# Nearest-neighbour upsampling by two: eight drains ahead of the second load, and a single row copied behind the other 53

## The chip, the core and the metric

The kernel runs on one core of a Trainium2 chip. The metric is the device time of one execution in microseconds (us). A lower time is better. The kernel before takes 197.13 us, the median of three runs (197.12 to 197.26).

## What is computed

The input `x` is float32 with the shape (16, 64, 64, 64), which is 16.78 MB. The output doubles height and width, so it has the shape (16, 64, 128, 128) and 67.11 MB. Every input value is written four times:

```
new_h, new_w = (h * scale_factor, w * scale_factor)      # scale_factor is 2
for i in range(new_h):
    for j in range(new_w):
        result[:, :, i, j] = x[:, :, i // scale_factor, j // scale_factor]
```

There is no arithmetic. The work is to bring 16.78 MB in, to repeat it fourfold on the chip, and to bring 67.11 MB out.

## The kernel before

Batch, channel and height are flattened to 65,536 input rows of 64 values. Each of the 128 partitions holds 512 of these rows. All 512 rows of a partition fit into the on-chip memory at once, together with some free space, in one tile called `mem`. The input part of it is `xt`.

**Loads.** SyncE issues three loads, cut at the rows 0, 32, 288 and 512 of each partition. They are called load 1 (1 MB), load 2 (8 MB) and load 3 (7 MB) below. `begin_before_barrier` moves load 1 ahead of the barrier with which the program starts. Ahead of each load stand as many SyncE drains as `PAUSES` says: none, two and forty. The drains wait for nothing here; they let time pass between two issues.

**Copies.** VectorE expands the rows in nine groups of `rows = [54, 38, 54, 60, 54, 62, 64, 62, 64]`. A copy reads a row of 64 values with every value taken twice and the row taken twice, and writes 256 values. So 53 rows are 13,568 values in each partition, and one row is 256. The first group is split: the single row 0 is copied on its own as soon as load 1 is there, and then the rows 1 to 53 in a second copy. Row 53 lies in load 2, so this second copy waits for load 2.

**Places.** Even groups are written at the start of `mem`. Odd groups are written further on, and they end over input rows that earlier copies have already read. Therefore the copy of the second group (38 rows) waits until the copies of the first group have finished, and each copy from the third on waits until the store of two groups earlier has landed.

**Stores.** Each group is one store. SyncE issues the first, the second and the last store, behind its three loads and in the same queue (q1 in the profile). ScalarE issues the other six (q10). The stores of the first group and load 3 are thus neighbours in one queue: the first store's data can only move when load 3's data has been moved, and only if the store has been issued early enough. It is issued when both copies of the first group are done.

**End.** `close_early` rewrites the closing instructions so that most of the clean-up happens before the last store has landed. The change does not touch it.

Of the kernel before, what the change touches and what calls it, by code (L numbers as in the profile page):

```python
# [7 lines left out]


EARLY = 1  # L10
PAUSES = (0, 2, 40)


def begin_before_barrier(nc):
# [140 lines left out]
@with_exitstack  # L155
def kernel(
    ctx: ExitStack,
    tc: tile.TileContext,
    x: bass.AP,
    scale_factor: int,  # L160
    out: bass.AP,
):
    nc = tc.nc
    nc.at_finalize(begin_before_barrier)
    nc.at_finalize(close_early)
    P = nc.NUM_PARTITIONS
    s = int(scale_factor)
    B, C, H, W = x.shape
    R = B * C * H // P
    fdt = x.dtype  # L170

    xp = x.rearrange("b c h w -> (b c h) w").rearrange("(p r) w -> p r w", p=P)
    op = out.rearrange("b c (h hd) w -> (b c h) (hd w)", hd=s).rearrange(
        "(p r) w -> p r w", p=P
    )

    rows = [54, 38, 54, 60, 54, 62, 64, 62, 64]
    GROW = s * s
    FREE = 79
    WF = FREE * GROW * W
    assert sum(rows) == R
    mem_pool = ctx.enter_context(tc.tile_pool(name="mem", bufs=1))
    LEAD = 32
    whole = mem_pool.tile([P, LEAD + WF + R * W], fdt, name="mem")
    mem = whole[:, LEAD:]  # L190
    xt = mem[:, WF:].rearrange("p (r w) -> p r w", r=R)

    HEAD = 32
    cuts = [0, HEAD, R // 2 + HEAD, R]
    for n, (lo, hi) in enumerate(zip(cuts, cuts[1:])):
        for _ in range(PAUSES[n]):
            nc.sync.drain()  # L199
        nc.sync.dma_start(out=xt[:, lo:hi], in_=xp[:, lo:hi])  # L200

    def expanded(r0, r1):
        return (
            xt[:, r0:r1].unsqueeze(2).unsqueeze(4).to_broadcast([P, r1 - r0, s, W, s])
        )

    r0 = 0
    before = (0, 0)
    for n, k in enumerate(rows):
        size = k * GROW * W  # L210
        at = 0 if n % 2 == 0 else WF + r0 * W - size
        assert at >= before[1] or at + size <= before[0]
        before = (at, at + size)
        u = mem[:, at : at + size].rearrange(
            "p (k a w b) -> p k a w b", k=k, a=s, w=W
        )
        k0 = 1 if n == 0 else 0
        if k0:
            nc.vector.tensor_copy(out=u[:, :k0], in_=expanded(r0, r0 + k0))  # L219
        nc.vector.tensor_copy(out=u[:, k0:], in_=expanded(r0 + k0, r0 + k))  # L220
        issuer = nc.sync if n in (0, 1, len(rows) - 1) else nc.scalar
        issuer.dma_start(out=op[:, r0 : r0 + k, :], in_=u)
        r0 += k
# [35 lines left out]
```

## Time and profile before

| what | value |
|---|---|
| time, median of three runs | 197.13 us |
| time of the profiled execution | 197.12 us |
| its span, first to last instruction | 195.8 us |
| VectorE busy | 76.9 us (39%) |
| bytes read and written | 16.78 MB and 67.11 MB |
| mean rate of the DMA engines over the span | 428 GB/s |
| first store issued at | 38.35 us |

The span is 1.3 us shorter than the time of the same execution; what lies outside it is before the first or after the last instruction of the profile. In the rows of the profile, DVE is VectorE, SPq and ACTq are the queues of SyncE and ScalarE, and L220 is a line of the kernel. A row of a DMA view gives what moved in a stretch of time. A packet is counted whole in the stretch in which it starts. That is a nuisance for short stretches where rates are wanted, and a help where starts are to be counted: the rate times the length of the stretch, divided by the size of a packet, is the number of packets that started in it. For load 3 a packet is one partition's 57,344 bytes, for the first store one partition's 55,296 bytes, and for loads and stores of 64 rows it is 65,536 bytes. Each of the 16 DMA engines moves the packets of 8 partitions, one behind the other.

### The profile page before, as it was taken

The page shows a single profiled execution, that of the slowest core. Times are in us where ns is not written, and L with a number is a line of the kernel's source. Part 1 is how long each engine was busy: PE and PEld are TensorE (multiplying, and loading weights), DVE is VectorE, ACT ScalarE, POOL GpSimd, SP SyncE. Part 2 cuts the span into 40 slices and gives each one's busy share as a digit, 9 for nine tenths or more (in the row PEclk, how much of TensorE's full clock was granted, in tenths as well). Part 3 has the DMA queues.
Part 4 walks back from the last instruction along what each step waited for, and adds up shares of the span by engine and source line. Part 5 has one row for each costly group of instructions (what it writes and reads, how often), then busy time and mean ns, then how long its engine had stood idle before and what let it go on. Part 6 is the DMA issues. An engine that isn't in the chain of part 4 may idle for free.

```text
span 195.8 us, 118 instructions
## 1 busy us (share of the span) xinstructions
DVE 76.9 (39%) x10; POOL 0.2 (0%) x4
## 2 busy tenths in 40 slices
DVE  0000099990029287059008805920690079000000
POOL 0000000000000000000000000000000000000000
DMA  9999989889898998999999899999999999999994
GB/s 428 428 428 428 402 375 562 375 361 531 373 435 382 517 407 361 542 402 402 402 503 441 361 542 415 415 415 415 428 428 428 428 415 454 537 475 422 428 428 214
DMA packets 1728, 83.89 MB, mean 428 GB/s; under 512 B 192, under 2 KB 192, under 8 KB 192
## 3 DMA queue, kind: packets, MB, share of 16 engines
q10 hardware_dynamic: 864, 46.66, 55.0%
q1 hardware_dynamic: 864, 37.22, 44.3%
HBM read 16.78 MB, written 67.11 MB: 428 GB/s over the span
## 4 chain that ended last, share of the span: by engine, by line
DMA 61%; DVE 24%; issue 0%; SPq 0%
DMA out_dram<-mem 49%; DVE mem L220 24%; DMA mem<-in_x_dram 12%; SPq L199 0%
## 5 line engine op out<-in xcount | busy, mean ns | idle before, releaser
L220 DVE COPY mem<-mem 128x13824 f32<-128x13824 f32 (+5 forms) x9 | 76.6, 8515 | 84.8 <-DMA out_dram<-mem 65.8
L219 DVE COPY mem<-mem 128x256 f32<-128x256 f32 x1 | 0.3, 293 | 4.7 <-DMA mem<-in_x_dram 4.7
L240 POOL MEMSET const-bfloat16-1.0<- 128x1 bf16 x1 | 0.1, 101 | 0.0
L240 POOL MEMSET const-uint8-127<- 128x1 uint8 x1 | 0.1, 101 | 0.0
L240 POOL MEMSET const-float32-1.0<- 128x1 f32 x1 | 0.1, 100 | 0.0
L240 POOL MEMSET const-float32-0.0<- 128x1 f32 x1 | 0.1, 98 | 0.2 <-issue 0.2
## 6 DMA issues: line engine op xcount, KB each, us to landing
out_dram<-mem ACTq DMA_DIRECT2D x2, 7936.0 KB, 31.6
out_dram<-mem ACTq DMA_DIRECT2D x2, 6912.0 KB, 23.7
out_dram<-mem ACTq DMA_DIRECT2D x1, 7680.0 KB, 26.1
mem<-in_x_dram SPq DMA_DIRECT2D x1, 7168.0 KB, 37.7
out_dram<-mem SPq DMA_DIRECT2D x1, 6912.0 KB, 19.1
out_dram<-mem SPq DMA_DIRECT2D x1, 4864.0 KB, 25.4
mem<-in_x_dram SPq DMA_DIRECT2D x1, 1024.0 KB, 4.7
mem<-in_x_dram SPq DMA_DIRECT2D x1, 23.1
```

What stands on the lines that cost most here:

```text
L219: nc.vector.tensor_copy(out=u[:, :k0], in_=expanded(r0, r0 + k0))
L220: nc.vector.tensor_copy(out=u[:, k0:], in_=expanded(r0 + k0, r0 + k))
L240: nc = _bacc.Bacc("TRN2", target_bir_lowering=False, num_devices=1)
```

## The change

Two things change. `PAUSES` goes from `(0, 2, 40)` to `(0, 8, 40)`, so SyncE runs eight drains ahead of load 2 instead of two. And in the first group the single row moves: the copy of 53 rows comes first and covers the rows 0 to 52, and the single row is now row 53, copied behind it.

```
-PAUSES = (0, 2, 40)
+PAUSES = (0, 8, 40)
...
-        k0 = 1 if n == 0 else 0
-        if k0:
-            nc.vector.tensor_copy(out=u[:, :k0], in_=expanded(r0, r0 + k0))
-        nc.vector.tensor_copy(out=u[:, k0:], in_=expanded(r0 + k0, r0 + k))
+        parts = ((0, k - 1), (k - 1, k)) if n == 0 else ((0, k),)
+        for a, b in parts:
+            nc.vector.tensor_copy(out=u[:, a:b], in_=expanded(r0 + a, r0 + b))
```

On VectorE the order of the first two copies is reversed. Before, at the start of VectorE's program (128x256 is the single row, 128x13568 the 53 rows; DMAHW0 and DMAHW1 are the semaphores of load 1 and load 2, DVE is VectorE's own):

```order
L219 COPY mem<-mem 128x256 [waits DMAHW0_49]
L220 COPY mem<-mem 128x13568 [waits DMAHW1_49]
L220 COPY mem<-mem 128x9728 [waits DVE_49]
L220 COPY mem<-mem 128x13824 [waits DMAHW3_49]
L220 COPY mem<-mem 128x15360 [waits DMAHW4_49,DVE_49]
```

The same place of the changed program:

```order
L219 COPY mem<-mem 128x13568 [waits DMAHW1_49,DMAHW0_49]
L219 COPY mem<-mem 128x256
L219 COPY mem<-mem 128x9728 [waits DVE_49]
L219 COPY mem<-mem 128x13824 [waits DMAHW3_49]
L219 COPY mem<-mem 128x15360 [waits DMAHW4_49,DVE_49]
```

The large copy now reads rows of both loads, so it waits for two semaphores where it waited for one; a copy with two waits stands behind a separate wait instruction that holds the first of them. The single row waits for nothing of its own and follows the large copy. All later copies, and the order on SyncE and ScalarE, are as before, apart from the six added drains on SyncE between load 1 and load 2.

## The prediction

> **What bounds the kernel now.** I read the page first, for the engines' shares.
>
> ```profile
> DVE 76.9 (39%) x10; POOL 0.2 (0%) x4
> DMA  9999989889898998999999899999999999999994
> HBM read 16.78 MB, written 67.11 MB: 428 GB/s over the span
> ```
>
> VectorE is idle most of the time. The DMA engines work in all slices, and 83.89 MB at 428 GB/s is the whole span. So the time can only change where the DMA engines run empty for a moment. With nothing lost in the middle, what the change can touch is the head of the program. The chain of waits, up to the first store:
>
> ```profile
> 0.73 0.05 issue
> 0.78 0.01 SPq L199
> 0.79 0.05 issue
> 0.83 0.01 SPq L199
> 0.84 0.05 issue
> 0.89 23.12 DMA mem<-in_x_dram
> 24.02 0.02 issue
> 24.04 14.30 DVE mem L220
> 38.34 0.02 issue
> 38.35 19.14 DMA out_dram<-mem
> ```
>
> Load 2 is issued at 0.89 us behind two drains, lands at 24.02, releases the copy of 53 rows, and the first store is issued at 38.35. Next the issues of DMAs, with the time to landing:
>
> ```profile
> mem<-in_x_dram SPq DMA_DIRECT2D x1, 7168.0 KB, 37.7
> out_dram<-mem SPq DMA_DIRECT2D x1, 4864.0 KB, 25.4
> ```
>
> ```profile
> 3.47 0.33 SPq L200 DMA_DIRECT2D mem<-in_x_dram  x1
> 43.62 0.34 SPq L222 DMA_DIRECT2D out_dram<-mem  x1
> ```
>
> Load 3 lands at 3.47 + 37.7 = 41.2, only 2.8 us after the first store's issue. Both are in one queue. Is the store there in time when load 3's data ends? Short windows answer it, since a packet counts where it starts (columns: stretch, length, DVE, POOL, clock, DMA share, GB/s):
>
> ```profile
> 38.26:38.50 0.24, 0.20 (x2) 0.00 (x0) 1.00 9.14 3823
> 38.50:40.46 1.96, 1.96 (x1) 0.00 (x0) 1.00 0.00 0
> 40.46:40.62 0.16, 0.16 (x1) 0.00 (x0) 1.00 9.61 4148
> 40.62:40.73 0.11, 0.11 (x1) 0.00 (x0) 1.00 0.00 0
> 40.73:40.84 0.11, 0.11 (x1) 0.00 (x0) 1.00 4.66 2011
> 192.64:192.82 0.18, 0.00 (x0) 0.00 (x0) 1.00 10.07 4369
> 192.82:192.91 0.09, 0.00 (x0) 0.00 (x0) 1.00 0.00 0
> 192.91:193.02 0.11, 0.00 (x0) 0.00 (x0) 1.00 5.50 2383
> ```
>
> First row: 3823 GB/s times 0.24 us is 16 packets of 57,344 bytes, the last of load 3, one on each engine, all started within 0.24 us. The store's first packets don't follow in the same spread: 4148 x 0.16 / 55,296 = 12 start by 40.62, then a hole, and 2011 x 0.11 = 4 start at 40.73 to 40.84. Four engines got the store late. They never make it up: at the end 12 of the last packets (65,536 bytes each) start by 192.82, and the same number of four, behind a hole, at 192.91 to 193.02. These four set the end. So for the late engines the store was ready only 2.38 to 2.49 us after its issue (40.73 - 38.35, 40.84 - 38.35), and **the first store's issue is on the path**: what delays it delays the end one for one, as long as load 3 doesn't end later too.
>
> **The change, part by part.** The copies by form:
>
> ```profile
> L220 DVE COPY mem<-mem 128x13824 f32<-128x13824 f32 x2 | 14.7, 7360 | 22.0 <-DMA out_dram<-mem 22.0
> L220 DVE COPY mem<-mem 128x13568 f32<-128x13568 f32 x1 | 14.3, 14287 | 19.0 <-DMA mem<-in_x_dram 19.0
> L220 DVE COPY mem<-mem 128x9728 f32<-128x9728 f32 x1 | 5.2, 5226 | 0.0
> L219 DVE COPY mem<-mem 128x256 f32<-128x256 f32 x1 | 0.3, 293 | 4.7 <-DMA mem<-in_x_dram 4.7
> ```
>
> *The copy of 53 rows* keeps its shape, at half the rate of its neighbours: 14.29 us before and after. It starts at load 2's landing in both, since load 1 is there by 4.7.
>
> *The single row* cost nothing before: it ran at 4.73, while VectorE waited for load 2. Now it stands between the large copy and the store. Its row says 0.29 us. The gap between two copies is 0.03, from the next start:
>
> ```profile
> 38.36 5.23 DVE L220 COPY mem<-mem 128x9728 f32<-128x9728 f32 x1
> ```
>
> That is 38.36 against an end of 24.04 + 14.29 = 38.33. But here a semaphore lies between the copies, and the moved row has none ahead of it. No row shows that case. The bounds are 0.32 (the row in full with its gap) and 0.13: the larger copies differ by 4096 values and 7360 - 5226 = 2134 ns, so 0.52 ns a value, and 256 values alone take 0.13. It can't be below that, for VectorE has to write them ahead of the store. I take 0.32, the value of the nearest rows. The Trainium skill, VectorE: DVE Perf Modes, section "The DRAIN you can't avoid", says that eight copies took the same time with a semaphore behind each as with one behind the last; by that the sum stays at 0.32. Its section "Two Vector instructions with no wait between them" says that a second instruction whose operands start in the same quadrants is not held until the first has finished; by that it would go towards 0.13. No row of this trace shows either.
>
> *The second wait* of the large copy. With one wait it starts 0.02 behind the landing (24.02 to 24.04). The copy that has a wait instruction ahead of it is the fifth:
>
> ```profile
> 69.10 8.16 DVE L220 COPY mem<-mem 128x15360 f32<-128x15360 f32 x1 [4.22 <-DMA out_dram<-mem]
> ```
>
> It waited for the second store, landed at 43.62 + 25.4 = 69.02, so it started 0.08 behind it, with an uncertainty of 0.05 since the 25.4 is rounded. I take a start 0.11 behind the landing, the upper half of that, since the wait and the copy are two instructions, and so 0.09 more than now; the bounds are 0.01 and 0.11. A gain is excluded, since nothing can start before the landing.
>
> *The six drains* cost SyncE 0.05 each (0.78 to 0.83), 0.32 in all. Load 2 is issued at 1.21 instead of 0.89, load 3 at 3.79. Does that reach the data? Load 2's first packets:
>
> ```profile
> 4.14:4.25 0.11, 0.00 (x0) 0.00 (x0) 1.00 5.52 2383
> 4.25:4.40 0.15, 0.00 (x0) 0.00 (x0) 1.00 12.13 5243
> ```
>
> These are 4 and 12 packets of 65,536 bytes, in one bunch from 4.14 to 4.40: no late group, load 1's data ends only then. By the store's 2.49 us, load 2 is ready at 0.89 + 2.49 = 3.38 now and at 3.70 then, 0.44 before it is needed. Load 3 has 20 us of cover. So I cost the drains at nothing; without load 1's cover they cost up to 0.32.
>
> Queued behind the moved row is the copy of 38 rows, which now starts at about 38.77 and ends at 44.0; its store isn't due until the first store's data is done at about 57. It stays covered.
>
> Sum: 0.32 + 0.09 = **0.41**. First store issued at 38.76, late packets at 41.14 to 41.25, the end 0.41 later: 197.12 + 0.41 = 197.53 for the profiled execution. That one is 0.01 below the median of the runs, so the forecast is 197.13 + 0.41 = **197.54 us**, 0.21% slower. A measurement of this kernel can tell about 0.2%, or 0.39 us. The forecast lies at this limit, and its own range is 0.36 to 0.46 (the wait between 0.05 and 0.11, the row and its gap between 0.31 and 0.35): 197.49 to 197.59.
>
> **The rivals.**
>
> *The moved row overlaps the large copy's end.* With no wait between them it costs 0.13 to 0.2. For: two instructions without a semaphore. Against: the 0.03 gap at 38.36 shows no overlap, though there a wait stood. Sum 0.13 + 0.09 = 0.22: 197.35 us, no change that can be told. This is where the second section named above leads.
>
> *The store is early enough anyway.* Load 1 was issued at 0.00 and its first bytes move at 1.0 to 2.0:
>
> ```profile
> 0.50:1.00 0.50, 0.00 (x0) 0.00 (x0) 1.00 0.00 0
> 1.00:2.00 1.00, 0.00 (x0) 0.00 (x0) 1.00 0.98 139
> 2.00:4.00 2.00, 0.00 (x0) 0.00 (x0) 1.00 1.02 430
> ```
>
> If a store needs no more than 1.7 us from issue to readiness, one issued at 38.76 is ready at 40.46, and load 3 hides the delay: 197.13 us. The hole at 40.62 to 40.73 then has another cause, such as the turn from loading to storing. Against: load 1 reaches its full rate only after 2.0. The Trainium skill, DMA: Bandwidth & Descriptors, section "Latency and other measured facts", gives about 600 ns to the first byte for such a DMA; by that this rival would hold, but nothing moves in this trace before 1.0.
>
> *The drains are on the path too.* If load 2 needs over 2.93 us from issue (4.14 - 1.21), its data comes late, and each further 0.1 costs 0.1, up to 0.32. Everything behind moves, and the store's delay comes on top: 0.41 + 0.32 = 0.73, 197.86 us. Against: no late group at 4.14. For: in that bunch a margin can't be seen, only worked out from another DMA.
>
> *Not slower: the drains help load 1.* Between 1.0 and 2.0 only 139 GB/s move against 430 afterwards, so (430 - 139) / 430 = 0.68 us are lost, just after load 2 is issued at 0.89 to 1.22. If preparing load 2 is what holds load 1's packets up, six more drains free them, and load 2 lands up to 0.68 earlier. The store is then issued at 38.35 + 0.41 - 0.68 = 38.08: 196.86 us. It decides from a gain of 0.41 on; with the row overlapped it would be 0.22 - 0.68 = -0.46, 196.67. Against: load 1 is alone in the chip at first, and a first packet has to wait for its data whatever stands behind it.
>
> That the change doesn't do what it says (the copy of 53 rows at the faster rate) I leave at no chance: its 53 rows are the same shape.
>
> **How the numbers follow.** The forecast 0.52; two thirds of its range of 0.36 to 0.46 lie above 0.39, so 0.36 slower and 0.16 the same. The overlap 0.12 and the early store 0.08, both the same. The drains on the path 0.18, slower. The drains that help 0.10, half faster (with the overlap), half the same. Faster 0.05, same 0.16 + 0.12 + 0.08 + 0.05 = 0.41, slower 0.36 + 0.18 = 0.54. The range takes in the early store, from 197.10 since runs of one kernel differ by some hundredths, and the drains on the path with the upper end of the wait, 197.95; it leaves out the 0.10 of the last rival.
>
> **What the changed profile would show.** Right: the copy of 53 rows starting 0.1 behind load 2's landing at about 24.0; 256 values at about 38.44, 0.29 long; the first store issued at 38.76; its first packets up to 41.25, with more than four engines late; the last packets 0.4 later. Overlap: the single row ends less than 0.25 behind the large copy. Early store: the store issued at 38.76, but the end unmoved. Drains on the path: load 2's first packets in two groups, and its landing at 24.3. Drains that help: more than 139 GB/s at 1.0 to 2.0, and a landing before 23.8. I am wrong altogether if the span changes while the first store's packets start where they did.

## The result, and the profile after

| kernel | median | runs | ratio to before (95% interval) |
|---|---|---|---|
| before | 197.12 us | 6 (197.02 to 197.26) | |
| changed | 197.95 us | 6 (197.69 to 198.26) | 1.0046 (1.0035 to 1.0056) |

The change makes the kernel slower by 0.83 us. The forecast was slower too, but by 0.41 us and, as the experiments show, for another reason. The runs of the changed kernel also spread over 0.57 us, where those of before lie within 0.24. The profiled execution took 198.23 us with a span of 196.9, so it shows one of the larger losses. Its chain of waits at the head:

```profile
1.15 0.05 issue
1.21 23.92 DMA mem<-in_x_dram
25.13 0.03 issue
25.16 0.02 DVEq L219
25.18 0.05 issue
25.23 14.50 DVE mem L219 x2
39.73 0.02 issue
39.74 18.86 DMA out_dram<-mem
```

Load 2 is issued 0.32 us later, as worked out, but it lands 1.11 us later, at 25.13 instead of 24.02. From there the steps are near the forecast's: 0.10 from the landing to the copy (25.13 to 25.23, with the separate wait in the rows between), and 14.50 for the two copies instead of 14.30 for one. The first store is issued at 39.74. So the large step is ahead of VectorE, in load 2. The short windows, read as before by the packets that start in them:

```profile
4.00:4.55 0.55, 0.00 (x0) 0.00 (x0) 1.00 4.31 1862
4.55:4.70 0.15, 0.00 (x0) 0.00 (x0) 1.00 1.39 437
6.45:7.00 0.55, 0.00 (x0) 0.00 (x0) 1.00 4.14 1787
7.00:7.85 0.85, 0.00 (x0) 0.00 (x0) 1.00 0.00 0
7.85:8.00 0.15, 0.00 (x0) 0.00 (x0) 1.00 1.01 437
40.46:41.10 0.64, 0.64 (x1) 0.00 (x0) 1.00 3.04 1296
41.10:41.80 0.70, 0.70 (x1) 0.00 (x0) 1.00 0.00 0
41.80:42.10 0.30, 0.30 (x1) 0.00 (x0) 1.00 0.43 184
192.80:193.40 0.60, 0.00 (x0) 0.00 (x0) 1.00 3.78 1638
193.40:194.00 0.60, 0.00 (x0) 0.00 (x0) 1.00 0.00 0
194.00:194.20 0.20, 0.00 (x0) 0.00 (x0) 1.00 0.76 328
```

Load 2's packets have 65,536 bytes. Their first ones start on fifteen engines by 4.55 (1862 x 0.55 / 65.5 is a little more, because a few small packets of load 1 are in the row too) and on one engine (437 x 0.15 / 65.5 = 1) at 4.55 to 4.70. The second packets tell more: 1787 x 0.55 / 65.5 = 15 start by 7.00, then nothing for 0.85 us, and the sixteenth at 7.85 to 8.00. The DMA share counts a packet whole where it starts, as the rate does, so it gives the time that a packet took: 1.39 x 0.15 x 16 engines = 3.3 us for the one at 4.55, and 1.01 x 0.15 x 16 = 2.4 us for the one at 7.85. So one engine of sixteen had its first packet of load 2 almost in time and lost about 1 us within it. Load 2 has landed only when its last engine is done, so this one engine delays its landing, the large copy and the first store. And it never catches up: the first store's packets start on fifteen engines by 41.10 and on one at 41.80 to 42.10; the last packets of the program start on fifteen by 193.40 and on one at 194.00 to 194.20. Before, the last ones started at 192.91 to 193.02. The difference of about 1.1 us is the difference of the spans, 196.9 against 195.8.

### The profile page after: what moved, and what is told of

It reads as the page before. It is cut to its first block, busy times and chain, and to the rows that moved or that the text cites. A ratio compares the mean times of both kernels' runs of the same rounds, so it can differ in the third digit from the quotient of the medians.

```text
span 196.9 us, 125 instructions
## 1 busy us (share of the span) xinstructions
DVE 76.8 (39%) x10; POOL 0.2 (0%) x4
## 4 chain that ended last, share of the span: by engine, by line
DMA 61%; DVE 24%; issue 0%; SPq 0%; DVEq 0%
DMA out_dram<-mem 49%; DVE mem L219 24%; DMA mem<-in_x_dram 12%; SPq L199 0%; DVEq L219 0%
## 5 line engine op out<-in xcount | busy, mean ns | idle before, releaser
L219 DVE COPY mem<-mem 128x13824 f32<-128x13824 f32 (+6 forms) x10 | 76.8, 7692 | 90.7 <-DMA out_dram<-mem 65.5
```

What stands on the lines that cost most here:

```text
L219: nc.vector.tensor_copy(out=u[:, a:b], in_=expanded(r0 + a, r0 + b))
```

## The experiments

Every ratio below is to the kernel before, run on the same chip, with its 95% interval. Edits are to the kernel before, where nothing else is said.

### Which half of the change costs

```
e1:  PAUSES = (0, 8, 40)                   # drains alone, single row in front
e2:  the changed kernel with PAUSES = (0, 2, 40)   # single row behind, alone
e3:  PAUSES = (0, 2, 46)                   # the six drains ahead of load 3
e4:  PAUSES = (0, 8, 40); cuts = [0, HEAD + 16, R // 2 + HEAD, R]
```

> The kernel before with the drains alone: eight ahead of load 2, single row still in front. Theory A (load 2's issue comes too late for the last DMA engine, which then lags to the end): most of the 0.83 us of the whole change, 197.6 to 198.2 us; one or two of the sixteen first packets of load 2 run 0.5 us or more behind the rest, and load 2 lands at 24.5 to 25.2. Theory B (the moved row carries the cost, as the prediction had it): 197.1 us, load 2 lands at 24.0.

> The changed kernel with two drains again: the single row behind the 53 rows alone. Theory A: load 2 lands at 24.0 in one bunch; the first store is issued about 0.37 us later than before and the time is 197.3 to 197.5 us. Theory B: it has all of the change, 197.95 us. If load 3 hides the store's delay: 197.1 us.

> The kernel before with the six added drains ahead of load 3 instead of load 2: the same number of instructions on SyncE, load 2 issued at 0.89 us as before, load 3 0.3 us later. Theory A: 197.1 us, no lagging engine. A rival C (the longer program costs, wherever the drains stand): about 197.6 to 198.

> Eight drains, single row in front, and load 1 made 48 rows instead of 32 (load 2 then 240 rows, load 3 unchanged): load 1's data lasts 1.2 us longer, so load 2 has more cover. Theory A: no lagging engine, load 2 lands at 24.0, about 197.1 us. If the drains cost in another way than through load 1's end, it stays at the time of the drains alone.

| run | median | range | ratio |
|---|---|---|---|
| e1, drains alone | 197.98 | 197.06 to 198.67 | 1.0040 (1.0028 to 1.0053) |
| e2, row behind alone | 197.06 | 196.98 to 197.15 | 0.9994 (0.9986 to 1.0003) |
| e3, drains ahead of load 3 | 197.14 | 197.02 to 197.39 | 0.9998 (0.9989 to 1.0007) |
| e4, drains and a longer load 1 | 197.11 | 197.02 to 197.52 | 1.0001 (0.9992 to 1.0009) |

The drains are the whole loss within the intervals, and the moved row costs nothing. The windows of e1 around the first and the second packets of load 2:

```profile
4.10:4.50 0.40, 0.00 (x0) 0.00 (x0) 1.00 6.48 2642
6.50:6.90 0.40, 0.00 (x0) 0.00 (x0) 1.00 5.37 2294
6.90:7.60 0.70, 0.00 (x0) 0.00 (x0) 1.00 0.00 0
7.60:7.85 0.25, 0.00 (x0) 0.00 (x0) 1.00 1.21 524
```

All sixteen first packets start by 4.50. Of the second ones fourteen start in time and two (524 x 0.25 / 65.5) about 1 us late. How many engines lag differs from profile to profile (one in the changed kernel, two here), which would explain the wide range of times. e3 has the same number of instructions on SyncE and no loss, so it isn't the longer program. e4 gives load 1 half as many rows again, so that its data lasts 1.2 us longer, and the loss is gone. Load 2's first packets (61,440 bytes there) in e4:

```profile
5.20:5.60 0.40, 0.00 (x0) 0.00 (x0) 1.00 4.98 2151
5.60:6.00 0.40, 0.01 (x1) 0.00 (x0) 1.00 0.71 307
```

Sixteen start (14 and 2), and none is stretched: (4.98 + 0.71) x 0.40 = 2.3 us each, which is 2.4 scaled to their bytes. So what holds load 2's first packets up in e1 is over, or doesn't arise, by the time at which they start here. That fits a wait at the head of the packet better than a slower engine; no view shows the inside of a packet.

e2 speaks against the prediction's reading of the first store. Its chain:

```profile
24.18 14.50 DVE mem L219 x2
38.67 0.02 issue
38.69 18.70 DMA out_dram<-mem
```

and its windows where the first store's packets start:

```profile
40.20:40.71 0.51, 0.51 (x1) 0.00 (x0) 1.00 4.02 1735
40.71:41.20 0.49, 0.49 (x1) 0.00 (x0) 1.00 0.00 0
```

The store is issued 0.34 us later than before, as the step-by-step sum would have it (0.20 for the row, 0.08 for the second wait, and a landing of load 2 that is 0.06 later in this execution), and yet all sixteen first packets (1735 x 0.51 / 55.3) start by 40.71. There is no late group of four.

### When load 2's issue hurts

```
e5:  PAUSES = (0, 5, 40)      e6:  PAUSES = (0, 16, 40)
e7:  PAUSES = (0, 28, 40)     e9:  PAUSES = (0, 40, 40)
e10: HEAD = 24                # load 1 of 24 rows, load 3 of 232
e11: EARLY = 2; PAUSES = (0, 0, 48)   # load 2 ahead of the barrier too
e12: PAUSES = (0, 8, 80)
e15: EARLY = 0; PAUSES = (0, 7, 40)   # load 1 behind the barrier
e16: EARLY = 0; PAUSES = (0, 14, 40)
```

> Single row in front, five drains ahead of load 2 (issued at about 1.05 us). Theory A (lateness: the later load 2's issue, the more engines find no work when load 1's data ends): between two drains and eight, 197.1 to 197.7 us, fewer lagging engines or smaller lags. Theory D (a collision: load 2's issue is harmful only while load 1's first packets are starting, 1.2 to 1.6 us): about 197.1 us.

> Single row in front, sixteen drains (load 2 issued at about 1.61 us). Theory A: more lagging engines than with eight, lags of 1.0 to 1.5 us, 198.2 to 198.8 us. Theory D: back towards 197.1 to 197.5 us.

> Single row in front, twenty-eight drains (load 2 issued at about 2.25 us, load 3 at 4.85). Theory A: all sixteen engines late, load 2 lands at 25.2 or later, 198.6 to 199.3 us. Theory D: load 1's first packets are over by then, 197.1 us.

> Single row in front, forty drains ahead of load 2 (issued at about 2.9 us). Theory A1 (every engine that runs out of work pays, and what it pays is set by the issue: 1.7 to 1.9 us from issue to full flow, as for load 1): all sixteen engines late together by about 0.6 us, load 2 lands at 24.6, 197.7 to 197.9 us and little spread. Theory A2 (load 2 needs 3 us or more from issue to its data in some engines, whenever it is issued): 199 us or more.

> Two drains as before, single row in front, but load 1 of 24 rows instead of 32 (load 2 of 256 rows as before, load 3 of 232): load 1's data ends 0.6 us earlier, load 2 is issued at 0.89 us as before. If the end of load 1's data is the deadline: one or more lagging engines, 197.4 to 198.1 us. If only the moment of load 2's issue matters: 197.1 us.

> Load 2 moved ahead of the barrier as load 1 is, with no drains before it (issued at about 0.4 us), and 48 drains ahead of load 3; single row in front. Load 2 gets 0.5 us more cover. Deadline theory: no lagging engine in any run, 197.1 us with a spread no wider than 0.3 us. If an issue close behind load 1's disturbs load 1: slower.

> Eight drains ahead of load 2, eighty ahead of load 3 instead of forty (load 3 issued at about 5.9 us). If the lagging engines are caused by load 2's lateness alone: as with eight and forty, 197.7 to 198.2 us. If load 3's issue, at about 3.8 us and thus close to load 2's start, is what holds them up: 197.1 us. If they are released only by the next issue: 199 us or more.

> Load 1 issued behind the barrier (about 0.75 us later than before), then seven drains, so that load 2 is issued 0.87 us behind load 1, the distance of the kernel before, but later in the program. If the distance to load 1 decides: load 2's first packets in one bunch, about 197.9 us (0.75 later for the barrier alone). If the time since the program's start decides: a lagging engine, 198.5 us or more.

> As the run before with fourteen drains: load 2 issued about 1.2 us behind load 1, the distance of the changed kernel. If the distance decides: one or more engines lag by 0.5 to 1.1 us, 198.5 to 199 us. If it is the time since the start: as with seven drains, about 0.75 us over before.

In order of the time by which load 2 is issued behind load 1:

| run | load 2 behind load 1 | median | range | ratio |
|---|---|---|---|---|
| e11 | 0.43 us | 197.07 | 196.97 to 197.31 | 0.9997 (0.9988 to 1.0005) |
| before | 0.89 us | 197.1 | | 1 |
| e5 | 1.04 us | 197.16 | 197.04 to 198.32 | 1.0008 (0.9997 to 1.0019) |
| e1 | 1.19 us | 197.98 | 197.06 to 198.67 | 1.0040 (1.0028 to 1.0053) |
| e12 | 1.19 us | 198.14 | 197.92 to 198.81 | 1.0056 (1.0042 to 1.0069) |
| e6 | 1.61 us | 198.12 | 197.91 to 198.36 | 1.0049 (1.0037 to 1.0061) |
| e7 | 2.22 us | 198.15 | 197.71 to 198.86 | 1.0053 (1.0037 to 1.0069) |
| e9 | 2.86 us | 197.81 | 197.79 to 198.10 | 1.0039 (1.0025 to 1.0052) |
| e10, short load 1 | 0.89 us | 197.61 | 197.38 to 197.81 | 1.0027 (1.0018 to 1.0035) |

By the medians the loss sets in between 1.04 and 1.19 us and then stays near 1 us; it doesn't grow with the delay. At 40 drains it is even smaller, with a narrow range apart from one run. The border isn't sharp: at 1.04 two of eleven runs took longer (197.57 and 198.32), and at 1.19 (e1) one of eleven lost nothing (197.06). The windows around the second packets of load 2 show that it isn't one thing. With 16 drains (e6), 28 (e7) and 40 (e9):

```profile
6.50:6.90 0.40, 0.00 (x0) 0.00 (x0) 1.00 0.00 0
6.90:7.50 0.60, 0.00 (x0) 0.00 (x0) 1.00 3.08 1311
7.50:8.10 0.60, 0.00 (x0) 0.00 (x0) 1.00 1.01 437
```

```profile
6.50:6.85 0.35, 0.00 (x0) 0.00 (x0) 1.00 5.18 2247
6.85:7.40 0.55, 0.00 (x0) 0.00 (x0) 1.00 1.10 477
```

```profile
6.40:6.85 0.45, 0.00 (x0) 0.00 (x0) 1.00 0.34 146
6.85:7.65 0.80, 0.00 (x0) 0.00 (x0) 1.00 2.84 1229
```

These are second packets, as in e1. Issued at 1.61, all sixteen are late (12 by 7.50 and 4 after that). Issued at 2.22, which is later, 12 are in time. Issued at 2.86, fifteen are late again, but none after 7.65. A packet of 65,536 bytes takes 2.4 us on an undisturbed engine (sixteen of them at the 430 GB/s of load 1), so, if the time is lost at the head of the first packet, a second packet at 8.0 stands for data that flows from about 5.6, which is 4.0 us behind the issue at 1.61; one at 7.65 for 5.2, which is 2.4 behind the issue at 2.86. Neither theory of the expectations explains all of this. Lateness alone (theory A) would have made e7 worse than e6, and in its profiled execution 12 of 16 engines were in time; that one is the fastest of its six, 197.71 us. That only a moment early in load 1 matters (theory D) would have brought 197.1 us back with 28 and 40 drains; it didn't. What the runs allow is both, by these estimates: an issue 1.2 to 1.6 us behind load 1's takes up to 4 us to become data on some engines, against at most 2.4 us for the one issued at 2.86, and what isn't covered by load 1's data is lost.

e12 shows that load 3's issue isn't part of it: with load 3 issued 2.5 us later, the lag of load 2 is as before. e10 moves the end of load 1's data 0.6 us closer to an unchanged issue. Its second packets of load 2:

```profile
5.80:6.35 0.55, 0.00 (x0) 0.00 (x0) 1.00 4.40 1907
6.35:7.20 0.85, 0.00 (x0) 0.00 (x0) 1.00 0.00 0
```

All sixteen (1907 x 0.55 / 65.5) start by 6.35, so each had its data by 6.35 - 2.4 = 3.95 or earlier, at most about 3.1 us behind the issue at 0.89. No engine lagged, though load 2 had less cover than in e1: its data was wanted 0.6 us earlier, for an issue 0.3 us earlier. The same working gives 4.0 to 4.2 us behind the issue for the two late engines of e1. This is against a reading by cover alone: an issue at 0.89 is ready sooner than one at 1.19. The loss of e10 lies elsewhere (below). e15 and e16 move load 1 and load 2 together by the 0.73 us that load 1 stands behind the start of the span then. With load 2 issued 0.92 us behind load 1 the time is 197.90 us (1.0039, 1.0025 to 1.0052), 0.78 us over before and so little more than the later start; with 1.29 us it is 198.70 us (1.0086, 1.0071 to 1.0102). Their chains:

```profile
1.65 23.21 DMA mem<-in_x_dram
24.86 0.02 issue
```

```profile
2.02 23.77 DMA mem<-in_x_dram
25.79 0.02 issue
```

Load 2 lands 0.93 us later for an issue that is 0.37 later. So it is the distance to load 1's issue that decides whether load 2 is held up, and not the time since the start of the program.

### When the first store's issue hurts

```
e8:  e2 with parts = ((0, k - 1), *[(k - 1, k)] * 7) for the first group
e13: k0 = 3 if n == 0 else 0
e17: e13, and ahead of the second group's copy
+            nc.vector.tensor_copy(out=mem[:, at : at + W], in_=xt[:, 400])
e18: e17 with k0 = 0
e14: the changed kernel with EARLY = 2; PAUSES = (0, 0, 48)
```

> Two drains, single row behind, and this single row copied seven times over (six of them waiting for the one before), so the first store is issued about 1.9 us later than with one, at about 40.6 us. If the store's issue were on the path from the start, as the prediction had it: 199.0 us. If the store needs 0.9 to 1.3 us from issue to its first packets and so had about 0.8 us to spare: 1.1 us lost, 198.1 us. If load 3 hides all of it: 197.1 us.

> The kernel before with three rows in front instead of one, so that the large copy has 51 rows and the first store is issued 0.53 us earlier, at about 37.83 us. As the prediction read it (four engines got the store too late): the late group goes, 196.9 us. If the store comes too early already and stretches load 3's last packets: all or most of the sixteen stretched by 0.3 us or more, 197.4 to 197.7 us.

> As the run with three rows in front (first store issued at about 37.9 us), but ahead of the second group's copy stands a copy of one row of load 3 into the same place, so that this copy starts only when load 3 has landed, at about 41.2 us. If the store is what stretches load 3's last packets: stretched as before, 197.4 to 197.7 us. If the second group's copy does it: none stretched, 197.0 us.

> The first group in one copy of 54 rows (the double rate, 7.36 us, so the first store is issued at about 31.5 us), the second group's copy again waiting for load 3. If an early store stretches load 3's last packets: all sixteen stretched at the end of load 3, 197.5 us or more. If a copy at the double rate beside a load does it: packets stretched at 24 to 31.5 us instead, about 197.1 to 197.7 us. If neither alone: 197.0 us.

> The changed kernel with load 2 ahead of the barrier (no drains before it, 48 before load 3) and the single row behind: the two versions that were not slower, together. No lagging engine at 4.1 to 4.5 us, no stretched packets at 40.5 us: 197.0 us, 0.05 to 0.1 us below before, which may not be told from no change.

| run | first store issued | median | range | ratio |
|---|---|---|---|---|
| e18 | 31.85 us | 198.34 | 198.20 to 198.58 | 1.0064 (1.0052 to 1.0077) |
| e13 | 37.91 us | 197.65 | 197.34 to 197.84 | 1.0024 (1.0014 to 1.0034) |
| e17 | 38.01 us | 197.73 | 197.53 to 197.89 | 1.0035 (1.0021 to 1.0048) |
| before | 38.35 us | 197.1 | | 1 |
| e14 | 38.65 us | 197.11 | 196.97 to 197.19 | 0.9998 (0.9989 to 1.0006) |
| e2 | 38.69 us | 197.06 | 196.98 to 197.15 | 0.9994 (0.9986 to 1.0003) |
| e8 | 40.67 us | 198.01 | 197.92 to 198.06 | 1.0042 (1.0029 to 1.0055) |

There is a valley. To the right of it the store is late, as the prediction feared. In e8:

```profile
40.67 0.35 SPq L221 DMA_DIRECT2D out_dram<-mem  x1
```

```profile
40.70:41.50 0.80, 0.80 (x1) 0.00 (x0) 1.00 0.00 0
41.50:41.70 0.20, 0.20 (x1) 0.00 (x0) 1.00 10.36 4424
```

All sixteen first packets (4424 x 0.20 / 55.3) start at 41.50 to 41.70, that is 0.83 to 1.03 us behind the issue, while load 3's data ended at 40.3 to 40.7, as it did in e2. So here a store that idle engines wait for needs about 1 us. By that, issued at 38.35, this store had about 1 us to spare, and at 38.69 still 0.5.

To the left the store comes too early. In e13 the last packets of load 3 start at their usual time, and the store's first packets start late:

```profile
38.20:38.70 0.50, 0.50 (x1) 0.00 (x0) 1.00 4.94 1835
40.46:40.72 0.26, 0.26 (x1) 0.00 (x0) 1.00 0.49 213
40.72:41.20 0.48, 0.48 (x1) 0.00 (x0) 1.00 4.00 1728
```

All sixteen packets of 57,344 bytes start by 38.70, as before and as in e2, but only one of the store's packets starts by 40.72 and fifteen after that. The last packets of load 3 have become longer. The share gives their mean: 4.94 x 0.50 = 2.5 us. In e8, where the store comes late, it is 4.23 x 0.50 = 2.1:

```profile
38.10:38.60 0.50, 0.50 (x2) 0.00 (x0) 1.00 4.23 1835
```

For the kernel before, the first row of short windows in the prediction gives 9.14 x 0.24 = 2.2 (2.19 against 2.12 in e8), so some packets were a little longer there too. Two things start at 37.91: the store, and the second group's copy on VectorE at twice the rate of the large copy. In e17 that copy has to wait for load 3 and starts at 41.79; the time is no better. In e18 the store is issued 6.5 us earlier than before and the copy waits as well:

```profile
38.40:39.30 0.90, 0.00 (x0) 0.00 (x0) 1.00 3.64 1019
40.40:41.75 1.35, 0.00 (x0) 0.00 (x0) 1.00 0.00 0
41.75:42.30 0.55, 0.00 (x0) 0.00 (x0) 1.00 3.73 1609
```

All sixteen of load 3's last packets start by 39.30 and the store's (1609 x 0.55 / 55.3 = 16) only from 41.75 on, with nothing in between. By the share they took 3.64 x 0.90 = 3.3 us on average. VectorE did nothing from 31.85 to the landing of load 3. So it is the store, waiting in the same queue right behind load 3, that stretches load 3's last packets, and the more the earlier it is issued. Whether a store in the other queue would do the same, no run shows. This also is where e10 seems to have lost its time: load 2 landed at 23.51 there, the store was issued at 37.85, and of its first packets one started by 40.72 and fifteen after that.

e14 joins the two edits that did no harm. It can't be told from before, and no version that was run is faster than before beyond its interval.

## Why the prediction was right or wrong, step by step

**That the head of the program decides** was right: a lag at the first store's start stays to the end. That the time can only change where DMA engines run empty was too narrow: the engine that lags here has a packet all the time, and this packet takes 3.3 us instead of 2.4. That the kernel became slower, as forecast, is luck, for the forecast's two terms are worth nothing (e2), and what costs is the part that it put at nothing.

**The six drains cost nothing** was wrong, and this is the step that failed. The issue did come 0.32 us later. But the step took the time from issue to data from the first store (2.49 us), used it for load 2 at any moment of issue, found a margin of 0.44 us, and bounded the loss by 0.32, the delay of the issue. Load 2 needed more than that on one or a few engines: the late engine's second packet at 7.85 to 8.00 stands, by the same estimate as above, for data from 5.4 to 5.6, over 4 us behind the issue at 1.21. Load 2 landed 1.11 us later. The loss isn't bounded by the delay either; an issue 0.3 us later cost 0.84 us (197.98 against 197.14). The rival "the drains are on the path too" had the right part of the change, at a chance of 0.18. Its sign, load 2's first packets in two groups, hardly shows (one first packet stands a little behind the others in the changed kernel, and all sixteen start by 4.50 in e1); the two groups are in the second packets. Its price, 0.41 + 0.32, came near the measured 0.83 by accident, since neither term holds. It expected a landing at 24.3 and the profile shows 25.13. The upper end of the range, 197.95, is called this rival with the upper end of the wait; that sum is 0.32 + 0.11 + 0.32 = 0.75 and gives 197.88. That the median of 197.95 came to lie right there is luck too.

**The first store's issue is on the path, one for one** was wrong, and in sign. The four engines on which the store's first packets started at 40.73 to 40.84 had not got the store too late; had it been so, e13 would have been faster and e2 slower. So 2.38 to 2.49 us wasn't the time that a store needs; e8 shows 0.83 to 1.03. e13, e17 and e18 show that an early store stretches load 3's last packets. That the four of the kernel before were mild cases of this fits the mean of 2.19 us there; the windows don't say which engines had the longer packets.

**The moved row at 0.32** was 0.20 (14.50 for both copies against 14.30), so the overlap that was a rival is real: the single row takes 0.28 by its own row and adds 0.20. This agrees with the Trainium skill, VectorE: DVE Perf Modes, section "Two Vector instructions with no wait between them", by which such a copy need not wait until the one ahead has finished. **The second wait at 0.09** was 0.08. Both delay the first store as worked out, by 0.28 instead of 0.41, and both are worth nothing here (e2), as the rival of the early store had it. What that rival needed, no more than 1.7 us from issue to readiness, is 0.83 to 1.03 in e8. The Trainium skill, DMA: Bandwidth & Descriptors, section "Latency and other measured facts", gives about 0.6 us to the first byte; the rows of e8 are longer, but under 1.7 as well.

**The drains help load 1** was wrong as to the time: an issue 0.46 us earlier (e11) changed nothing, and a later one helped in no run. One of its signs did appear, 172 GB/s at 1.00 to 2.00 in the changed kernel against 139, but load 2 landed later and not earlier.

**Left open** is why an issue 1.2 to 1.6 us behind load 1's takes so long to become data on some engines. At that time load 1's own first packets are under way (139 GB/s between 1.0 and 2.0 before). That the two disturb each other is a guess; no run separates it. Open too is why an issue at 2.22 holds up fewer engines than one at 1.61 or 2.86.

## What to carry to other kernels

Where a kernel keeps all DMA engines busy, look for single engines that lag: in this one a transfer landed when its slowest engine was done, and a lag of one engine near the start stayed to the end. Count packets in short windows at each seam between two transfers, read from the share how long they took, and don't read from a late start alone whether the next transfer came too late or too early; move its issue both ways. And before you space out the issue of a program's second transfer, try it close behind the first (0.43 and 0.89 us did no harm here) or with a larger first transfer to cover it (e4).

## What the runs showed of the hardware that I had not expected

A load issued 1.19 us behind the first one lost about 1 us within its first packet on two of sixteen engines (e1). One issued at 1.61 reached its second packets late on all sixteen, while one issued at 0.43 or 0.89 was in time on all. A store queued right behind a load in the same queue stretched the load's last packets from 2.1 to 3.3 us on average when it was issued 6.5 us earlier than in the kernel before, and left no trace when it was issued at 38.69, 1.5 to 2 us ahead of the end of the load's data.
